# Two of seven products of a Strassen-Winograd input projection split once more, with operands kept from the first phase

## The chip, the core and the metric

The kernel runs on one core of a Trainium2 chip. TensorE (PE, with its weight loads listed as PEld) multiplies and writes PSUM; VectorE (DVE) and ScalarE (ACT) do elementwise work and are the ones that read PSUM here; GpSimd (POOL) does a few small things and issues some DMAs; SyncE (SP) only issues DMAs. The metric is the device time of one execution in microseconds (us), taken as the median of the runs.

## What is computed

The reference, cut to the one layer that runs (`DEPTH` is 1): 4096 tokens of 1024 channels, all in float32.

```python
normed = rms_norm(x, norm_w)
u, gate = jnp.split(normed @ in_w, 2, axis=-1)          # in_w is 1024 x 2048
ug = u.reshape(b, s, 4, 256)
pooled = stack([trailing_mean(ug[:, :, g], w) for g, w in enumerate((2, 4, 8, 16))]) - ug
mixed = einsum('bsgc,gcd->bsgd', pooled, group_w) + group_b
h = x + (mixed.reshape(b, s, 1024) * scale * silu(gate)) @ out_w
out = rms_norm(h, final_norm_w)
```

The kernel folds each group's map `group_w` into `in_w` beforehand, so that one projection gives the mapped values and the gates.

## The kernel before, in words

**Arithmetic.** Each matrix product is done on float32 numbers that are split into a high and a low part (`split`, line 154: ACT copies the high part, DVE subtracts it to get the low part), and three matmuls high·high, high·low, low·high make one product (`mm3`, line 576). On top of it each 2x2 block product is done by the Strassen-Winograd scheme in seven block products: P1 = A11 B11, P2 = A12 B21, P6 = S2 T2, P7 = S3 T3, P5 = S1 T1, P4 = A22 T4, P3 = S4 B22. The S are sums of blocks of A (the normalised tokens, transposed), the T sums of blocks of B (the weights).

**Stages.** There are three, each a row of steps, and a step is one product (line 960). First input phase "a": four blocks of 1024 tokens, seven products each, for the first two groups (values and gates). Second input phase "b": the same four blocks for the last two groups. Output phase "o": eight blocks of 512 tokens, seven products each. In the input phases one product is 48 matmuls (`product_in`, line 587): two halves h of 256 rows of the inner dimension, four column tiles ct of 128, two kk of 128 rows, three matmuls of 128x128 weights against 512 tokens. One (h, ct) pair, six matmuls, I call a unit. Four PSUM banks ("x") take P1, P2 and later P7, P4, the other four ("y") take P6, P5, P3.

**Operands of A.** Phase a loads the transposed tokens (`load_x`), normalises them, forms the sums (`form_in`, line 514), splits them into `op` tiles (`split_halves`, line 470), and stores the operands of P1, P2, P7 and P4 to DRAM (`sd`). Phase b loads these four back (`load_saved`, line 490) and forms the sums for P6, P5 and P3 again on DVE (`form_in` and `form_s4`): six subtractions or additions of 128x1024 a block.

**Order.** The program is written in the order of the steps; at step n the loop at line 1204 loads operands up to three steps ahead, forms sums two ahead, splits one ahead (`split_reach`), does the pooling that has come due (`pool`, line 628), runs the product (`run`, line 994), and evicts it (`evict_in`, line 710). Eviction of P1 is a copy by ACT from the x banks to the y banks, of P2, P6, P7, P3 a copy to SBUF, of P5 and P4 an addition by DVE. Each engine works through its own list in order. `tc.high_priority()` moves instructions forward in it, `tc.issue_after(...)` puts them behind another instruction. Buffers of SBUF come from a list of eleven `st` and eight `vt` tiles of 128x1024, the oldest free one first; whoever takes one waits for its last reader, DMAs included. Weights lie in `w[i][h]`; those of phase b are formed during the last block of a and the first of b (`form_wb`, `split_wb`); `make_wo` (line 320) forms those of the output phase during phase b and stores them (`wod`), `load_w` (line 328) loads and splits them in b's last block. `save_t3` (line 274), run in block 2 of phase a, loads four weight blocks, subtracts and stores T3.

Of the kernel before, what the change touches and what calls it, by code (L numbers as in the profile page):

```python
# [36 lines left out]
class Slots:  # L37
# [4 lines left out]
    def __init__(self, tiles):  # L42
        self.free = deque((0, t) for t in tiles)
        self.used = {}

# [16 lines left out]
def kernel(  # L62
# [48 lines left out]
    ops = [mem.tile([P, 4 * H], F32R, tag=f"op{i}", name=f"op{i}") for i in range(4)]  # L111
    st = Slots([mem.tile([P, D], F32, tag=f"st{i}", name=f"st{i}") for i in range(NS)])
# [41 lines left out]
    def split(dst, src):  # L154

        latest_split[1] = copy(dst[:, 0], src).ins
        latest_split[0] = sub(dst[:, 1], src, dst[:, 0].bitcast(F32)).ins
# [10 lines left out]
    wvd = [dram.tile([P, 2, H], F32, name=f"wvd{k}") for k in range(4)]  # L168
    t3d = [dram.tile([P, 2, H], F32, name=f"t3d{h}") for h in range(2)]
    wod = {  # L170
        i: [dram.tile([P, 2, H], F32, name=f"wod{i}_{h}") for h in range(2)]
        for i in range(P1, P7 + 1)
# [4 lines left out]
            for i in (P1, P2, P7, P4)  # L177
# [7 lines left out]
    nc.vector.memset(eps, EPS)  # L185
    scrap = const.tile([P, 1], F32, name="scrap")
# [133 lines left out]
    def make_wo(h):  # L320
        us = {}
        for n in range(2):
            for kh in range(2):
                us[kh, n] = load_rows(out_w, 4 * kh + 2 * h, n * H)
                scale_rows(us[kh, n], pair(scale_c, h, kh))
        store_weights(wod, h, us[0, 0], us[1, 0], us[0, 1], us[1, 1])

    def load_w(src, i):
        for h in range(2):
            u = take()  # L330
            nc.sync.dma_start(out=u, in_=src[i][h])
            split(w[i][h], u)
# [128 lines left out]
    turn = [0]  # L461

    def next_op(pattern, **sizes):
        t = ops[turn[0] % 4]
        turn[0] += 1
        return t.rearrange(pattern, **sizes)
# [3 lines left out]
    def split_halves(us, saved=None, by_pool=False):  # L470
        ts = []
        for h, u in enumerate(us):
            t = next_op("p (s a b) -> p s a b", s=2, a=2)
# [24 lines left out]
    def swapped(q, b):  # L498
        return q == 0 and b > 0

    def load_in(q, b, i):
        s = xs[b]
        if i == P1:
            s["11"] = load_saved(b, P1) if q else load_x(b, 0, 0)
        elif i == P2:
            s["12"] = load_saved(b, P2) if q else load_x(b, 0, 1)
        elif i == P7 and swapped(q, b):
            s["21"] = load_x(b, 1, 0)
        elif i == P6:
            if not swapped(q, b):  # L510
                s["21"] = load_saved(b, P7) if q else load_x(b, 1, 0)
            s["22"] = load_saved(b, P4) if q else load_x(b, 1, 1)

    def form_in(q, b, i):

        s = xs[b]
        if i in (P1, P2):
            if q == 0:
                for u in s["11" if i == P1 else "12"]:
                    normalize(b, 0, u)  # L520
        elif i == P7 and swapped(q, b):
# [4 lines left out]
        elif i == P6:  # L526
            s["2"] = [take() for _ in range(2)]
            for h in range(2):
                if q == 0:
                    normalize(b, 1, s["22"][h])  # L530
                sub(s["2"][h], s["22"][h], s["21"][h])
            if q == 0:
                give(rstd.pop(b))
# [6 lines left out]
    def split_in(q, b, i):  # L540
        s = xs[b]
        key = {P1: "11", P2: "12", P6: "2", P7: "21", P5: "11", P4: "22", P3: "12"}[i]
        later = q == 0 and b == 0 and i in (P1, P2)
        t = split_halves(s[key], None if q or later else sd[b].get(i), b == 0)
        if later:
            stores.extend(zip(sd[0][i], s[key]))
        if i == P6 and (q or b):
            form_s4(b)
        if i == P6 and swapped(q, b):
            for u in s.pop("21"):  # L550
                give(u)
        elif i not in (P1, P2, P6) and not (i == P7 and swapped(q, b)):
# [33 lines left out]

    def product_in(i, t, sets, by_bank, between=None, behind=None):
        ps = sets[bank_of[i]]
# [3 lines left out]
        for n, (h, ct) in enumerate(halves):  # L592
            if between and n in between:
                between[n]()
            c = slice(ct * P, (ct + 1) * P)
            with tc.issue_after(behind) if behind and n == 1 else nullcontext():
                for kk in range(2):
                    mm3(
                        ps[ct],
                        (w[i][h][:, 0, kk, c], w[i][h][:, 1, kk, c]),  # L600
                        (t[h][:, 0, kk], t[h][:, 1, kk]),
# [720 lines left out]
```

## Time and profile before

| | |
|---|---|
| median of 3 runs | 916.59 us (915.73 to 917.37) |
| the profiled execution | 917.32 us, of which the span from first to last instruction is 915.6 us |
| granted TensorE clock | 0.998 |
| busy: PE, DVE, ACT | 904.4 us (99%), 703.5 us (77%), 457.5 us (50%) |
| matmuls and weight loads | 4212 each |
| DMA | 177.02 MB, mean 193 GB/s |

Start times in the trace count from the start of the span. By the first start of every 48th matmul phase a begins at 33.4 us, phase b runs from 328.3 to 618.4 us and phase o until 908.6 us. One step of phase a or b takes 10.36 us.

### The profile page before, as it was taken

The numbers are of one execution on the slowest core, as the hardware profiler recorded it, in microseconds if no ns is written. First come the engines' busy times: TensorE is split into PE (matmuls) and PEld (weight loads), VectorE is DVE, ScalarE is ACT, GpSimd is POOL, SyncE is SP. The second block draws the span as 40 slices with busy tenths as digits, with TensorE's granted clock in tenths as the row PEclk, the third lists the DMA queues.
The fourth block names the chain that finished last, engine by engine and source line by source line (L and its number), as shares of the span: only waits on it lengthen the run. The fifth ranks groups of instructions, "written<-read, shape, count | busy, mean of one in ns | idle before, by whom it ended". The sixth has DMA issues, their size and how long they took to land.

```text
span 915.6 us, 11210 instructions
## 1 busy us (share of the span) xinstructions
PE 904.4 (99%) x4212; PEld 789.0 (86%) x4212; DVE 703.5 (77%) x769; ACT 457.5 (50%) x741; POOL 52.6 (6%) x130
## 2 busy tenths in 40 slices
PE   9999999999999999999999999999999999999996
PEld 7788888888888888888888888888888888888886
DVE  3898994894699997586696589589978677676675
ACT  7869447447345565246345546654423424324333
POOL 0023201001100000000000000000101101001010
PEclk9999999999999999999999999999999999999999
DMA  9986865666756635016614725745746536356122
GB/s 340 401 320 195 316 236 166 214 230 197 264 198 241 250 146 200 24 47 238 244 47 160 257 87 194 246 161 184 252 165 227 163 135 230 128 194 216 37 92 93
DMA packets 66518, 177.02 MB, mean 193 GB/s; under 512 B 6048, under 2 KB 23840, under 8 KB 66464
## 3 DMA queue, kind: packets, MB, share of 16 engines
q1 hardware_dynamic: 59888, 154.78, 47.9%
q10 hardware_dynamic: 4176, 13.65, 3.8%
q0 software_dynamic: 2400, 7.88, 2.5%
q8 instruction: 33, 0.54, 0.2%
q14 instruction: 21, 0.17, 0.1%
HBM read 115.45 MB, written 60.83 MB: 193 GB/s over the span
## 4 chain that ended last, share of the span: by engine, by line
PE 88%; DMA 5%; DVE 3%; ACT 2%; issue 1%; SPq 0%; DVEq 0%; ACTq 0%
PE bank L581 88%; DMA early<-in_wut 2%; DMA st<-in_x 1%; DMA st<-wvd 1%; DMA st<-in_xt 1%; DVE op L146 1%; DMA t3d<-st 1%; PE bank L374 0%; DVE st L146 0%; DVE st L149 0%; ACT early L408 0%; ACT op L152 0%; DVE st L143 0%; DVE vt L143 0%; DVE vt L146 0%
## 5 line engine op out<-in xcount | busy, mean ns | idle before, releaser
L581 PE MATMUL bank<-op,w 128*128 128x512 f32 x2688 | 581.8, 379 | 2.3 <-DVE op L146 1.5
L581 PEld LDWEIGHTS bank<-op,w 128*128 128x128 f32 x2688 | 507.6, 189 | 75.7 <-DVE op L146 2.3
L581 PE MATMUL bank<-w,op 128*128 128x512 f32 (+1 forms) x1356 | 290.3, 377 | 0.0
L581 PEld LDWEIGHTS bank<-w,op 128*128 128x128 f32 x1356 | 254.6, 189 | 35.8
L146 DVE TENSOR_TENSOR op<-st,op 128x1024 fp32r<-128x1024 f32 x127 | 154.6, 1221 | 75.6 <-ACT op L152 75.5
L152 ACT ACTIVATE op<-st 128x1024 fp32r<-128x1024 f32 x127 | 133.1, 1052 | 143.8 <-PE bank L581 128.5
L152 ACT ACTIVATE vt<-bank 128x512 f32<-128x512 f32 x100 | 56.8, 593 | 49.3 <-PE bank L581 42.4
L152 ACT ACTIVATE op<-vt 128x1024 fp32r<-128x1024 f32 x39 | 40.9, 1055 | 78.8 <-PE bank L581 65.7
L924 DVE TENSOR_TENSOR st<-bank,st 128x512 f32<-128x512 f32 x60 | 41.1, 687 | 29.8 <-PE bank L581 29.4
L146 DVE TENSOR_TENSOR st<-st,st 128x1024 f32<-128x1024 f32 x35 | 42.5, 1221 | 19.3 <-DMA st<-sd 8.6
L146 DVE TENSOR_TENSOR op<-vt,op 128x1024 fp32r<-128x1024 f32 x39 | 47.5, 1222 | 9.5 <-ACT op L152 9.5
L194 POOL TENSOR_SCALAR oms<-oss 128x2 f32<-128x2 f32 x14 | 9.2, 658 | 600.0 <-ACT st L813 593.9
L152 ACT ACTIVATE bank<-bank 128x512 f32<-128x512 f32 x48 | 27.8, 580 | 30.7 <-PE bank L581 27.1
L146 DVE TENSOR_TENSOR w<-st,w 128x1024 fp32r<-128x1024 f32 x21 | 25.5, 1221 | 12.4 <-ACT w L152 12.3
L662 DVE TENSOR_TENSOR_SCAN vt<-vt,bf 128x512 f32<-128x512 f32 x28 | 34.5, 1269 | 0.2 <-ACT vt L152 0.2
L143 DVE TENSOR_TENSOR vt<-bank,vt 128x512 f32<-128x512 f32 (+1 forms) x51 | 33.2, 678 | 1.6 <-PE bank L581 1.6
L924 DVE TENSOR_TENSOR vt<-bank,vt 128x512 f32<-128x512 f32 (+1 forms) x37 | 24.8, 673 | 12.0 <-PE bank L581 11.7
L152 ACT ACTIVATE w<-st 128x1024 fp32r<-128x1024 f32 x21 | 21.9, 1053 | 17.9 <-PE bank L581 14.9
L149 DVE TENSOR_TENSOR st<-st,vt 128x1024 f32<-128x1024 f32 x23 | 27.2, 1219 | 3.1 <-DMA st<-in_xt 3.1
L684 DVE SCALAR_TENSOR_TENSOR vt<-vt,vt 128x1024 f32<-128x1024 f32 x24 | 29.1, 1214 | 0.0
L152 ACT ACTIVATE st<-bank 128x512 f32<-128x512 f32 x30 | 17.5, 595 | 22.7 <-PE bank L581 10.8
L817 DVE SCALAR_TENSOR_TENSOR st<-st,ors,st 128x1024 f32<-128x1024 f32 x17 | 21.4, 1281 | 6.1 <-POOL ors L212 6.1
(130 smaller groups left out, 556.0 us busy)
## 6 DMA issues: line engine op xcount, KB each, us to landing
st<-in_x SPq DMA_DIRECT2D x36, 512.0 KB, 5.0
st<-in_xt SPq DMA_DIRECT2D x29, 512.0 KB, 6.6
st<-sd SPq DMA_DIRECT2D x29, 512.0 KB, 5.0
sd<-st ACTq DMA_DIRECT2D x23, 512.0 KB, 3.7
vt<-in_x SPq DMA_DIRECT2D x21, 512.0 KB, 5.1
st<-yd SPq DMA_DIRECT2D x19, 512.0 KB, 4.3
yd<-vt SPq DMA_DIRECT2D x18, 512.0 KB, 2.8
out<-st SPq DMA_DIRECT2D x17, 512.0 KB, 3.6
```

The source lines that it names most:

```text
L143: nc.vector.tensor_tensor(out=dst, in0=a, in1=b, op=ALU.add)
L146: return nc.vector.tensor_tensor(out=dst, in0=a, in1=b, op=ALU.subtract)
L149: nc.vector.tensor_tensor(out=dst, in0=a, in1=b, op=ALU.mult)
L152: return nc.scalar.activation(dst, src, func)
L194: nc.gpsimd.tensor_scalar(out=ms, in0=ss, scalar1=1.0 / D, scalar2=EPS, op0=ALU.mult, op1=ALU.add)
L581: latest[0] = nc.tensor.matmul(ps, a, b, start=start and n == 0, stop=stop and n == 2, skip_group_check=True).ins
L662: nc.vector.tensor_tensor_scan(s[:, j, at:end], v[:, j, at:end], v[:, j, at - win : end - win], sums_of[j] if sums_of else 0.0, ALU.add, A ...
L684: nc.vector.scalar_tensor_tensor(out=s[:, :, at : at + H], in0=s[:, :, at : at + H], scalar=1.0 / win, in1=v[:, :, HIST:], op0=ALU.mult, o ...
L817: nc.vector.scalar_tensor_tensor(out=us[j], in0=us[j], scalar=rs[:, j : j + 1], in1=fw[0], op0=ALU.mult, op1=ALU.mult,)
L924: partial["added"] = nc.vector.tensor_tensor(out=dst, in0=src, in1=dst, op=ALU.add).ins
```

## The change

Phase a stores the operands of all seven products; phase b loads all seven, two steps ahead, and `form_in` is left to phase a. `op` becomes a list of eight half-size tiles, so that high and low part lie in tiles of their own. In blocks 1 to 3 of phase b the products P1 and P7 (`INNER`) are no longer 48 matmuls: the 512x512x512 product is itself done as seven products of 256x256x256, in the order P1, P6, P2, P7, P5, P4, P3 (called inner P1 and so on here), each 12 matmuls of 128x128 weights against 256 tokens. Their intermediate sums are copied by ACT between halves of the x banks (`carry`), and one that can't be accumulated goes through DVE. The matmuls of an inner product's step are interleaved with the second half of the step before it (P3 or P6), as `fill`. The seven weight operands of each of the two are formed during phase a (blocks 1, 2) and block 0 of phase b, stored to DRAM, and loaded by POOL's queue into the memory of `w[P1]`, `w[P7]` and three `st` tiles, which are taken out of the list from block 0 of phase b until P7 of its last block. Stores of weights, and of `yd` in phase b, are kept in a list `due` and issued at the start of the next step. The diff, cut to its core:

```diff
-    ops = [mem.tile([P, 4 * H], F32R, ...) for i in range(4)]
+    ops = Slots([mem.tile([P, 2 * H], F32R, ...) for i in range(8)])
...
     def split_in(q, b, i):
         s = xs[b]
+        if q:
+            us = s[i]
+            if is_inner(b, i):
+                inner.update(us=us, sums={}, ops={})
+                with tc.high_priority():
+                    split_inner(M_ORDER[:4])
+                return None
...
+    M_ORDER = (P1, P6, P2, P7, P5, P4, P3)
+    def split_inner(ms):
...
+            if m == P6:
+                add(sums_in[P5], q[0, 1], q[1, 1])
+                sub(sums_in[P6], sums_in[P5], q[0, 0])
+            elif m == P7:
+                sub(sums_in[P7], q[0, 0], q[0, 1])
+            elif m == P3:
+                sub(sums_in[P3], q[1, 0], sums_in[P6])
...
+            split((by_side(ts[m][:, 0]), by_side(ts[m][:, 1])), src)
...
+    def mm_inner(m, banks_of, j, th):
+        t, wm = inner["ops"].pop(m), inner["w"][M_ORDER.index(m)]
+        for c in range(2):
+            ps = banks_of[2 * j + c][:, th * 256 : (th + 1) * 256].rearrange(...)
+            for kk in range(2):
+                for n, (sw, sr) in enumerate(((0, 0), (0, 1), (1, 0))):
+                    latest[0] = nc.tensor.matmul(ps, wm[:, sw, kk, cols_of], ..., start=False, ...)
+        ops.give(t)
+    def clear_inner(i, sets):
+        with tc.high_priority():
+            for v in part(sets[bank_of[i]], 0, 0):
+                copy(v, zero.to_broadcast([P, 256]))
+    def inner_product(i, sets, fill):
+        v11, v12, v21, v22 = part(ps, 0, 0), part(ps, 1, 0), part(ps, 0, 1), part(ps, 1, 1)
+        def carry(dst, src):
+            with tc.high_priority():
+                for c in range(2):
+                    inner["copied"] = copy(dst[c], src[c]).ins
+        mm_inner(P1, ps, 0, 0)
+        carry(v12, v11)
+        fill.pop(0)()
+        fill.pop(0)()
+        with tc.high_priority():
+            split_inner(M_ORDER[5:])
+        mm_inner(P6, ps, 1, 0)
+        carry(v21, v12)
+        fill.pop(0)()
+        mm_inner(P2, ps, 0, 0)
+        mm_inner(P7, ps, 0, 1)
+        u3 = inner["tiles"][0][:, 0]
+        carry(v22, v21)
+        carry([u3[:, 0], u3[:, 1]], v21)
+        fill.pop(0)()
+        mm_inner(P5, ps, 1, 1)
+        for c in range(2):
+            sub(u3[:, c], v22[c], u3[:, c])
+        mm_inner(P4, ps, 0, 1)
+        mm_inner(P3, ps, 1, 0)
+        for c in range(2):
+            add(v12[c], v12[c], u3[:, c])
...
+    def load_wi(i, ms):
+        for m in ms:
+            nc.gpsimd.dma_start(out=wi[i][m], in_=wid[i][m].bitcast(F32R))
+    def store_wi(i, src):
+        behind, after = latest_split[0], evicted[0]
+        for m, b in src.items():
+            u = take("p (s a b) -> p s a b", s=2, a=2)
+            r = u.bitcast(F32R)
+            with tc.issue_after(behind):
+                with tc.issue_after(after):
+                    copy(r[:, 0], b)
+                sub(r[:, 1], b, u[:, 0])
+            due.append((wid[i][M_ORDER.index(m)], u))
...
+        elif inner_step(n):
+            evict_in(b, 1, i, sets)
+        elif inner_step(n + 1):
+            t = split_up.pop(n)
+            clear_inner(next_i, sets)
+            for ct in range(4):
+                unit(i, t, sets, 0, ct)
+            give_ops(t[0])
+            with tc.high_priority():
+                split_inner(M_ORDER[4:5])
+            inner_product(next_i, sets, [lambda ct=ct: unit(i, t, sets, 1, ct) for ct in range(4)])
...
+            with tc.issue_after(inner["copied"]):
+                evict_in(b, 1, i, sets)
...
-        return 3 if kind == "a" and i == P6 else 4 if kind == "o" else 3
+        return 4 if kind == "o" else 3 if kind == "a" else 2
...
+    WI_PLAN = {
+        ("a", 1, P2): [(P1, 0)], ("a", 1, P6): [(P1, 1)], ("a", 1, P4): [(P1, 2)],
+        ("a", 2, P1): [(P1, 3)], ("a", 2, P7): [(P1, 4)],
+        ("b", 0, P6): [(P7, 0)], ("b", 0, P7): [(P7, 1)], ("b", 0, P5): [(P7, 2)],
+        ("b", 0, P4): [(P7, 3)], ("b", 0, P3): [(P7, 4)],
+    }
...
+        store_due()
```

`WI_PLAN` names the step behind which a part of the weights is formed: part 0 loads the raw blocks, part 1 makes four differences on DVE and stores them, parts 1 to 4 split and store the seven operands (`store_wi`). The output phase's weights are loaded one step before `split_w` splits them, and `make_wo` moves from behind P5 to behind P4, its loads staying behind P5.

More of the change, by code (lines that the diff above doesn't have):

```diff
@@ L44, in __init__, with retire, extend @@
         self.used = {}
+        self.tags = {}
+    def retire(self, n):
+        return [self.tags.pop(id(self.free.popleft()[1])) for _ in range(n)]
+    def extend(self, tiles):
+        for t, tag in tiles:
+            self.tags[id(t)] = tag
+            self.free.append((Slots.clock, t))
     def age(self):
@@ L460, with next_op, give_ops @@
     xs = [{} for _ in range(NB)]
[L461 to L466, printed above, removed]
+    def next_op(a):
+        return tuple(
+            ops.take(lambda t: t.rearrange("p (a b) -> p a b", a=a)) for _ in range(2)
+        )
+    def give_ops(ts):
+        for u in ts:
+            ops.give(u)
     first_saves = []
@@ new lines, in part @@
+    def part(ps, j, th):
+        return [ps[2 * j + c][:, th * 256 : (th + 1) * 256] for c in range(2)]
+    def clear_inner(i, sets):
[3 more added lines that the diff above has]
+    def inner_product(i, sets, fill):
+        ps = sets[bank_of[i]]
+        inner["w"] = wi[i]
+        v11, v12, v21, v22 = part(ps, 0, 0), part(ps, 1, 0), part(ps, 0, 1), part(ps, 1, 1)
[25 more added lines that the diff above has]
+            add(v12[c], v12[c], u3[:, c])
+        give(inner["tiles"][0])
@@ new lines, in store_wi, with raw_wi @@
+    def store_wi(i, src):
[8 more added lines that the diff above has]
+            due.append((wid[i][M_ORDER.index(m)], u))
+    def raw_wi(i):
+        formed["raw"] = []
+        for h in range(2):
+            if i == P1:
+                formed["raw"].append(load_rows(in_w, 2 * h, D + H))
+            else:
+                formed["raw"].append(take())
+                nc.sync.dma_start(out=formed["raw"][-1], in_=t3d[h])
@@ L632, in pool @@
         end = HIST + H
+        befores = small.tile([P, 4], F32, tag="before", name=f"bf{b}_{q}_{half}")
         for g in range(2):
@@ L1137 @@
         split_up[2] += split_halves([s["2"][h]])
+    stores.extend(zip(sd[0][P6], s["2"]))
     give(rstd.pop(0))
```

270 lines of the change are left out of this document (215 added, 55 removed).

## The prediction

> **What bounds the kernel now.** First the page's shares and its chain:
>
> ```profile
> PE 904.4 (99%) x4212; PEld 789.0 (86%) x4212; DVE 703.5 (77%) x769; ACT 457.5 (50%) x741; POOL 52.6 (6%) x130
> PE 88%; DMA 5%; DVE 3%; ACT 2%; issue 1%; SPq 0%; DVEq 0%; ACTq 0%
> ```
>
> Then the waits of PE alone, and PE's timeline, which starts a new row at each idle gap:
>
> ```profile
> PE bank L581 <- DVE op L146: 1.5, 2, 1.0
> PE bank L581 <- ACT w L224: 0.7, 1, 0.7
> ...
> 256.76 25.60 PE L581 MATMUL bank<-op,w 128*128 128x512 f32 x116 [0.96 <-DVE op L146]
> ...
> 459.83 100.53 PE L581 MATMUL bank<-op,w 128*128 128x512 f32 x465
> ```
>
> The reader is to see that TensorE is the bound. In the product line it waits 2.2 us in all, of which 0.96 us lies before 256.76, where phase a's last block begins. In 100 us of phase b it doesn't wait once. So a matmul less is time gained, and every wait put on PE is time lost; all else is worth nothing unless it makes PE wait.
>
> **PE's own work.** The tail of the kernel has both sizes of matmul, each with new weights, in two pieces of the PE timeline; their single durations are in the groups kept apart by shape:
>
> ```profile
> 899.91 5.99 PE L581 MATMUL bank<-w,op 128*128 128x512 f32 x27
> 905.74 2.84 PE L581 MATMUL bank<-w,op 128*128 128x256 f32 x24
> ...
> L581 PE MATMUL bank<-w,op 128*128 128x512 f32 x1332 | 287.7, 379 | 0.0
> ...
> L581 PE MATMUL bank<-w,op 128*128 128x256 f32 x24 | 2.8, 275 | 0.0
> ```
>
> The step from one matmul to the next is (5.99 − 0.379) / 26 = 0.2158 us at 512 tokens and (2.84 − 0.275) / 23 = 0.1115 us at 256. The weight load, which isn't shorter for 256, doesn't set the pace. A product of 48 costs 48 x 0.2158 = 10.36 us; seven inner products of 12 cost 84 x 0.1115 = 9.37 us. Gain 0.99 us each, six of them (P1 and P7, blocks 1 to 3): **−5.95 us**. All other matmuls stay.
>
> **Waits inside an inner product.** It is a chain: PE, a copy or subtraction in PSUM, PE again. Prices, and the busy time of the two steps that belong to it (P3 and P1: rows 1, 3, 5; P6 and P7: rows 2, 4, 6):
>
> ```profile
> L152 ACT ACTIVATE op<-st 128x1024 fp32r<-128x1024 f32 x127 | 133.1, 1052 | 143.8 <-PE bank L581 128.5 <-DVE st L149 14.8 <-DVE st L143 0.2
> L146 DVE TENSOR_TENSOR st<-st,st 128x1024 f32<-128x1024 f32 x35 | 42.5, 1221 | 19.3 <-DMA st<-sd 8.6 <-DMA st<-wvd 6.1 <-ACT st L232 4.3
> L152 ACT ACTIVATE bank<-bank 128x512 f32<-128x512 f32 x48 | 27.8, 580 | 30.7 <-PE bank L581 27.1 <-DVE st L146 3.6
> L844 ACT ACTIVATE st<-st 128x512 f32<-128x512 f32 x4 | 2.5, 632 | 7.1 <-DVE st L924 5.3 <-issue 1.9
> L149 DVE TENSOR_TENSOR st<-st,st 128x512 f32<-128x512 f32 x2 | 1.4, 682 | 0.0
> L924 DVE TENSOR_TENSOR vt<-bank,vt 128x256 f32<-128x256 f32 x2 | 0.8, 420 | 0.0
> L844 ACT ACTIVATE st<-vt 128x256 f32<-128x256 f32 x2 | 0.8, 408 | 0.0
> ...
> core 0: us, PE busy (x) PEld busy (x) DVE busy (x) ACT busy (x) POOL busy (x), PEclk, DMA share, GB/s
> 390.50:411.20 20.70, 20.70 (x97) 18.12 (x97) 17.59 (x23) 9.44 (x14) 0.00 (x0) 1.00 0.13 52
> 421.60:442.30 20.70, 20.70 (x97) 18.12 (x97) 12.34 (x11) 11.06 (x17) 0.00 (x0) 1.00 0.83 308
> 463.00:483.70 20.70, 20.70 (x98) 18.12 (x97) 17.21 (x17) 10.85 (x24) 0.00 (x0) 1.00 0.13 51
> 494.10:514.80 20.70, 20.70 (x97) 18.12 (x97) 8.85 (x8) 13.11 (x20) 0.00 (x0) 1.00 0.59 209
> 535.50:556.20 20.70, 20.70 (x98) 18.12 (x97) 19.01 (x19) 12.16 (x26) 0.00 (x0) 1.00 0.31 102
> 566.60:587.30 20.70, 20.70 (x98) 18.12 (x97) 14.90 (x13) 12.48 (x17) 0.00 (x0) 1.00 0.72 255
> ```
>
> Count from the first matmul of inner P1, with 1.34 us an inner product and 1.29 us a unit. The copies are priced by the 408 ns ACT row of 128x256; it reads SBUF, but at 128x512 the PSUM row (580) and the SBUF row (632) lie together. Inner P1 ends at 1.34, its results come about 0.16 later (275 ns less one step). Two copies take it to 2.3; two units cover until 3.9: spare 1.6. Inner P6 ends at 5.3, copies at 6.2; one unit covers until 6.6, where inner P2 starts: spare 0.4. Inner P7 ends at 9.2, the first two copies at 10.2; one unit covers until 10.5, where inner P5 starts: spare 0.3. The next two copies end at 11.0, inner P4 needs them at 11.9. Inner P5's last result comes at 12.0; DVE's two subtractions of 420 ns end at 12.9, inner P3 starts at 13.2: spare 0.3 if it has to wait for them. So nothing waits if ACT and DVE are free at the instant. Neither is preemptive: a 1.05 us copy or 1.22 us subtraction that has just begun overruns the spare by 0.7 or 0.9 us.
>
> How full are they? DVE gets, per inner product, seven low parts and four sums at 682 ns and four PSUM operations at 420: 7.5 + 1.7 = 9.2 us, for the two low parts of 1.22 us before: +6.7 us. In return the sums for P6, P5, P3 go, six of 1.22 us a block; two of them lie in each window. So each window gains 4.3 us of DVE work and shrinks to 10.36 + 9.37 = 19.73 us. The P6–P7 windows come to 16.6, 13.2 and 19.2: they fit. The P3–P1 windows come to 21.9, 21.5 and 23.3: over by 2.2, 1.8 and 3.6. About 10 us in them is pooling, which nobody awaits soon and which can slide into the steps around; DVE's order decides. I take 0.5 us of PE wait for each inner P1 (between none and the whole excess) and 0.13 for each inner P7: **+1.9 us**. ACT gains seven high parts at 632 ns and ten copies at 408, less two at 1,052: +6.4 us; its fullest window is then 19.5 of 19.7 (494.1, with weight scaling that the change puts a step later), others 16 to 19. That is in the same 1.9 us.
>
> What stands behind a waiting instruction: behind ACT's carry copies the high parts of the next product and P3's or P6's eviction, so DVE's low parts too; behind DVE's two subtractions the low parts of the next product. Those have five units of cover, as the second half of an operand is needed only after four units. Behind inner P3 come DVE's two additions and ACT's copies of P1 to the y banks: P2's third unit needs the third bank 2.6 us after inner P3 ends, and 0.16 + 0.42 + 0.58 is 1.2 us. Covered.
>
> The bank matters here. No row of this trace has two engines in two halves of one bank. The Trainium skill, PSUM — Partial Sum Buffer, section "PSUM bank collisions raise a hardware error", says that two engines may not be in one bank and partition quadrant at a time, at different addresses either, and that access has to be guarded by bank. By that rule inner P3, which writes the left halves of two banks, has to wait for DVE's reading of their right halves, and inner P2 for the copies into its own banks; without it only data would bind, and inner P3 wouldn't wait for DVE at all. The sum above goes by that; without it the waits of the inner P1s would be those for carry copies alone, by my estimate half, and the time about 0.8 us lower.
>
> **Phase a and the DMAs.** In transfers of 512 KB: 24 more stores (P6, P5, P3; four blocks, two halves), 24 more loads, 14 weight stores, 12 for raw blocks and differences, 26 weight loads by POOL: 100, or 52 MB on 177.
>
> ```profile
> 109.20:181.80 72.60, 72.60 (x338) 63.58 (x337) 56.55 (x58) 41.21 (x66) 5.18 (x14) 1.00 0.63 217
> 181.80:254.30 72.50, 72.50 (x337) 63.48 (x336) 50.75 (x53) 37.85 (x61) 6.01 (x14) 1.00 0.65 224
> ...
> 328.30:400.80 72.50, 72.50 (x338) 63.48 (x337) 54.54 (x59) 33.79 (x46) 0.00 (x0) 1.00 0.27 97
> 400.80:473.40 72.60, 72.60 (x338) 63.58 (x337) 52.07 (x51) 35.17 (x67) 0.00 (x0) 1.00 0.44 167
> ...
> 223.20:233.60 10.40, 10.40 (x50) 9.11 (x49) 1.36 (x2) 6.83 (x12) 0.77 (x2) 1.00 0.98 284
> 233.60:243.90 10.30, 10.30 (x49) 9.01 (x48) 7.23 (x10) 1.75 (x5) 2.19 (x5) 1.00 0.91 307
> ...
> 222.43 5.11 DMA t3d<-st
> 227.62 5.75 DMA st<-wvd
> ...
> 235.14 7.25 DMA st<-in_xt
> ...
> st<-sd SPq DMA_DIRECT2D x29, 512.0 KB, 5.0
> ...
> SPq L696 <- DVE vt L692: 87.1, 8, 35.1
> ```
>
> Phase b has room: block 1 adds 6 operand loads and up to 10 of weights, 8.4 MB in 72 us or 116 GB/s on 167, under the 308 that a stretch above shows. A load lands in 5.0 us and is now issued two steps ahead, 20 us; inner P7's last weights, loaded once inner P1 has done with the three tiles, have P2 and half of P6 as cover, 15 us for three transfers. I price them at nothing; a load that did come late would cost PE its lateness. SP stood up to 35 us behind a `yd` store (last row); moving those and the weight stores to the next step's start takes such waits away from operand loads, hidden before too: nothing. Forming the weights costs DVE 11 x 0.68 = 7.5 us and ACT about as much, in blocks with 16, 22 and 18 us of DVE idle: nothing.
>
> Phase a is tighter. Six more stores a block are 3.1 MB in 72.5 us, 43 GB/s on 217 to 233. The place is before 256.76: T3's round trip through DRAM and then the next block's tokens run one after another at DMA shares of 0.98 and 0.91. Into those 21 us fall the stores of P5 and P3, four transfers or 2.1 MB on 6.1 that they move now. Between −0.96 (the gap closes as buffers come in another order) and the stretch of the legs quoted by a third, 18.1 x 0.34 = +6.2 us; I take **+0.5 us**, near the low end, since P5's pair goes out before the worst leg.
>
> **The sum.** 917.32 − 5.95 + 1.9 + 0.5 = 913.8 for an execution like the profiled one. That one is 0.73 us above the median of the runs, so **913.0 us**.
>
> **Rivals.**
> *DVE becomes the bound at inner P1 (slower).* Place: DVE's two subtractions between inner P5 and inner P3, and the low parts ahead of them, behind pooling in DVE's order. Price: the whole excess, 2.2 + 1.8 + 3.6 = 7.6 us, with 0.4 for the inner P7s and 0.5 for phase a: 917.32 − 5.95 + 8.5 − 0.73 = 919.1. It decides from 0.99 us of wait per inner product; at half the excess the kernel is back where it was. For: the three windows above. Against: pooling is free to move, and before this change DVE was at 19.01 of 20.7 in one window and PE didn't wait.
> *Phase a's stores delay the tokens of block 3.* At the full 6.2 instead of 0.5: 913.0 + 5.7 = 918.7. For: DMA is full there, and PE already waits 0.96. Against: what goes out at 235 to 242 is one pair.
> *Everything is hidden.* 917.32 − 5.95 − 0.73 = 910.6; with the 0.96 gap gone, 909.7. For: every spare above is positive.
> *Something else is late*, weights through POOL's queue or buffers (three of eleven `st` tiles are gone): about 921, one wait of some 4 us in each of two blocks.
> That it doesn't do less on PE is no rival: 84 matmuls at the step measured in the tail.
>
> **Chances.** Forecast 0.58 (its own range 911 to 915; a twentieth of it ends within 0.2%), all hidden 0.08, DVE 0.18 (0.13 slower, 0.05 near the old time), phase a 0.12 (half and half), something else 0.04. The measurement can tell about 0.2%, 1.8 us: faster is under 914.8, slower over 918.4. Faster 0.55 + 0.08 = 0.63; same 0.03 + 0.05 + 0.06 = 0.14; slower 0.13 + 0.06 + 0.04 = 0.23. Range 910.0 to 920.5: it leaves out part of "all hidden" and the ends of the slower rivals, about 0.15.
>
> **What would show it.** Right: line 581 counts 288 matmuls fewer at 512 tokens, 504 new ones at 256 with a step near 0.11 us; PE's waits in phase b under 2 us, on carry copies and on DVE's subtraction; the gap before the last block of phase a within 1 us of what it was. Wrong: pieces of PE's timeline that end in phase b at inner P3 or P5 with over 1 us each (DVE), or a longer gap near 256 us that a DMA ended (phase a); a step of over 0.12 us for 256 tokens would take the gain itself.

## The result, and the profile after

The change makes the kernel slower: 950.78 us (median of 4 runs, 949.10 to 951.85) against 916.40 us, a ratio of 1.0373 [1.0354, 1.0392]. The forecast was 913.0 us. The profiled execution took 950.23 us, its span 948.4 us, at a mean granted clock of 0.987 (0.998 before); DMA moved 229.52 MB, 52.5 MB more, as counted.

The page's engine line and its chain of the changed kernel:

```profile
PE 909.3 (96%) x4428; PEld 795.2 (84%) x4428; DVE 723.6 (76%) x846; ACT 491.8 (52%) x849; POOL 71.1 (7%) x162
PE 59%; DVE 18%; DMA 12%; ACT 6%; issue 4%; SPq 0%; ACTq 0%; DVEq 0%
```

PE has 216 matmuls more (504 small ones for 288 large ones), but it isn't 99% busy any longer, and a third of the chain now runs through DVE, DMA and ACT. Where this happens is seen when the span is cut at the phases' first matmuls. First the kernel before (phase a's blocks 1 to 3, then phase b), then the changed one, with the three stretches of these phases in which the granted clock stood at half (columns: the stretch, its length, busy time of PE, PEld, DVE, ACT, POOL, granted clock, DMA share, GB/s):

```profile
109.20:328.30 219.10, 218.11 (x1010) 190.37 (x1009) 177.87 (x185) 117.72 (x186) 11.19 (x28) 1.00 0.64 225
328.30:618.40 290.10, 290.10 (x1346) 254.04 (x1345) 215.25 (x210) 147.64 (x252) 0.00 (x0) 1.00 0.44 157
```

```profile
108.40:336.70 228.30, 221.39 (x1009) 190.81 (x1009) 180.94 (x193) 120.02 (x195) 13.83 (x28) 0.99 0.78 277
336.70:651.40 314.70, 291.55 (x1561) 259.37 (x1560) 233.66 (x279) 179.85 (x350) 14.01 (x26) 0.97 0.72 254
...
230.85:234.26 3.41, 2.86 (x7) 2.32 (x8) 2.36 (x2) 3.41 (x6) 0.57 (x1) 0.50 0.75 256
428.82:435.65 6.83, 4.65 (x11) 3.71 (x12) 5.25 (x8) 3.08 (x11) 0.55 (x1) 0.50 0.64 227
602.90:613.14 10.24, 4.06 (x15) 3.70 (x16) 8.47 (x12) 3.89 (x6) 0.00 (x0) 0.50 0.56 200
```

Length less PE's busy time is PE's idle time. Phase b was never idle and is now idle for 314.70 − 291.55 = 23.15 us; its busy time, which should have fallen by 5.95, rose by 1.45. Phase a went from 0.99 to 6.91 us idle, and its busy time rose by 3.28 for the same matmuls. Together 23.15 + 1.45 + 5.92 + 3.28 = 33.8 us; the executions differ by 32.9. Phase o is as it was.

Of the busy time that is too long, 7.40 in b and 3.28 in a, about half is the clock. The last three rows show it: around PE's three longest waits the granted clock stands at 0.50 for 20.48 us in all, and PE is busy in 2.86 + 4.65 + 4.06 = 11.57 us of them. At half clock half of that is lost, about 5.8 us; while PE waits, the low clock costs nothing. Another 2.6 us come from how busy time is counted: the last matmul ahead of a wait counts with 0.379 us instead of its step of 0.2158, or with 0.275 instead of 0.1115, 0.163 more at each of the 16 waits in the two phases. The remaining 2.3 us, in which starts slip by less than shows as a gap, were not taken apart. So a long wait on PE costs more than itself.

The waits of PE in the changed kernel (engine, tile and line that waited, what ended it: us in all, times, longest), and the pieces of PE's timeline where phase b loses most; a piece's idle time stands ahead of it:

```profile
PE bank L706 <- ACT op L162: 10.8, 2, 8.3
PE bank L619 <- ACT bank L162: 8.6, 2, 7.5
PE bank L619 <- ACT st L162: 4.3, 3, 2.9
```

```profile
405.52 1.50 PE L706 MATMUL bank<-op,w 128*128 128x256 f32 x12
...
431.00 15.49 PE L619 MATMUL bank<-op,w 128*128 128x512 f32 x60 [7.55 <-ACT bank L162]
446.33 1.50 PE L706 MATMUL bank<-op,w 128*128 128x256 f32 x12
...
494.90 0.49 PE L706 MATMUL bank<-op,w 128*128 128x256 f32 x2 [2.50 <-ACT op L162]
...
576.83 1.60 PE L706 MATMUL bank<-op,shared_st 128*128 128x256 f32 x12 [0.70 <-DVE st L156]
...
609.08 0.79 PE L706 MATMUL bank<-op,w 128*128 128x256 f32 x2 [8.30 <-ACT op L162]
```

The first row says that PE's own gain is there: 12 matmuls at 256 tokens in 1.50 us, (1.50 − 0.275) / 11 = 0.111 us a step. Then come one wait of 7.55 us in block 1, one of 2.50 in block 2 and one of 8.30 in block 3, none at the place that I had named (inner P3 behind DVE's subtraction, where 0.70 stands). From here on "product P1" and "product P7" are the two that are done as seven, and "inner P3" and the like are the small products within one.

**The wait of block 1.** SyncE's waits from 400 to 421 us, its next two operand loads and their times to landing, then DVE and ACT:

```profile
SPq L796 <- DVE vt L948: 14.2, 2, 12.2
...
418.20 1.23 SPq L526 DMA_DIRECT2D vt<-sd  x2
...
DMA to landing us min/median/max: 7.6/8.5/9.3
```

```profile
420.04 1.22 DVE L156 TENSOR_TENSOR op<-st,op 128x1024 fp32r<-128x1024 f32 x1
428.03 0.69 DVE L153 TENSOR_TENSOR st<-vt,st 128x512 f32<-128x512 f32 x1 [6.77 <-issue]
...
429.85 0.43 DVE L153 TENSOR_TENSOR bank<-bank,st 128x256 f32<-128x256 f32 x1
```

```profile
425.86 1.06 ACT L162 ACTIVATE op<-vt 128x1024 fp32r<-128x1024 f32 x1 [4.82 <-DMA vt<-sd]
...
430.37 0.58 ACT L162 ACTIVATE bank<-bank 128x512 f32<-128x512 f32 x1 [2.77 <-DVE bank L153]
```

Read from the end: PE's unit at 431.00 waits for ACT's copy of P1 out of its bank (430.37), that copy for DVE's first addition in the bank (429.85), and that addition stands in DVE's list behind a sum of 128x512 at 428.03, one of product P7's, which `split_inner` put there with high priority. DVE did nothing for 6.77 us before it. The profile names no releaser ("issue"); the two operand loads issued from 418.20 on fit. The first landed after 7.6 us, at 425.84, and released ACT's copy at 425.86; the second, issued at 418.64, landed after 9.3 us, at 427.95, and the sum starts at 428.03. In SP's list they stand behind two stores of `yd`, which waited 14.2 us for pooling on DVE (line 948). Product P7 itself starts only at 446.33: counted to the matmul the load had 28 us, but DVE was free for the sum at 421.26, 2.6 us after the issue.

**The wait of block 3.** ACT and DVE ahead of 609.08:

```profile
589.78 1.57 ACT L162 ACTIVATE op<-st 128x1024 fp32r<-128x1024 f32 x2 [7.88 <-DMA st<-sd]
...
607.19 1.83 ACT L162 ACTIVATE op<-st 128x512 fp32r<-128x512 f32 x3 [5.37 <-DVE st L153]
```

```profile
590.87 1.83 DVE L156 TENSOR_TENSOR op<-st,op 128x1024 fp32r<-128x1024 f32 x2 [8.57 <-ACT op L162]
592.62 3.63 DVE L918 TENSOR_TENSOR_SCAN vt<-vt,bf 128x512 f32<-128x512 f32 x3
...
604.20 2.36 DVE L156 TENSOR_TENSOR w<-st,w 128x1024 fp32r<-128x1024 f32 x2
606.47 0.69 DVE L153 TENSOR_TENSOR st<-st,st 128x512 f32<-128x512 f32 x1
```

A load is late again (ACT idle 7.88 us, DVE 8.57 behind it). What DVE couldn't do then it does afterwards: from 592.62 pooling and the splits of the output phase's weights, and only at 606.47 the sum from which ACT and PE take an operand of product P7.

### The profile page after: what moved, and what is told of

Read it like the earlier page. It is cut to its first block, busy times and chain, and to the rows that moved or that the text cites. A ratio compares the mean times of both kernels' runs of the same rounds, so it can differ in the third digit from the quotient of the medians.

```text
span 948.4 us, 12129 instructions
## 1 busy us (share of the span) xinstructions
PE 909.3 (96%) x4428; PEld 795.2 (84%) x4428; DVE 723.6 (76%) x846; ACT 491.8 (52%) x849; POOL 71.1 (7%) x162
## 2 busy tenths in 40 slices
DMA packets 81180, 229.52 MB, mean 242 GB/s; under 512 B 7648, under 2 KB 25440, under 8 KB 81120
## 4 chain that ended last, share of the span: by engine, by line
PE 59%; DVE 18%; DMA 12%; ACT 6%; issue 4%; SPq 0%; ACTq 0%; DVEq 0%
PE bank L619 53%; PE bank L706 5%; DVE op L156 3%; DVE st L159 2%; DVE vt L153 2%; DVE st L156 2%; DMA early<-in_wut 2%; DMA st<-in_x 2%; DMA st<-wvd 2%; DMA sd<-st 2%; DVE st L153 1%; ACT op L162 1%; DVE vt L940 1%; DVE vt L156 1%; DMA st<-sd 1%
## 5 line engine op out<-in xcount | busy, mean ns | idle before, releaser
L619 PE MATMUL bank<-op,w 128*128 128x512 f32 x2400 | 530.6, 382 | 18.0 <-ACT bank L162 8.6
L619 PEld LDWEIGHTS bank<-op,w 128*128 128x128 f32 x2400 | 454.0, 190 | 87.2 <-ACT bank L162 9.2
L156 DVE TENSOR_TENSOR op<-st,op 128x1024 fp32r<-128x1024 f32 (+1 forms) x129 | 138.2, 1081 | 63.5 <-ACT op L162 51.7
L162 ACT ACTIVATE op<-st 128x1024 fp32r<-128x1024 f32 (+1 forms) x129 | 120.3, 942 | 124.4 <-PE bank L619 64.8
L162 ACT ACTIVATE op<-vt 128x1024 fp32r<-128x1024 f32 (+1 forms) x52 | 51.5, 995 | 81.2 <-PE bank L619 66.1
L156 DVE TENSOR_TENSOR op<-vt,op 128x1024 fp32r<-128x1024 f32 (+1 forms) x52 | 59.1, 1140 | 7.9 <-ACT op L162 7.6
L162 ACT ACTIVATE bank<-bank 128x512 f32<-128x512 f32 (+1 forms) x84 | 40.2, 488 | 35.6 <-PE bank L706 18.9
L706 PE MATMUL bank<-op,w 128*128 128x256 f32 x288 | 37.2, 282 | 12.2 <-ACT op L162 10.8
L706 PEld LDWEIGHTS bank<-op,w 128*128 128x128 f32 x288 | 36.1, 197 | 14.8 <-ACT op L162 11.6
L156 DVE TENSOR_TENSOR st<-st,st 128x1024 f32<-128x1024 f32 (+1 forms) x28 | 30.2, 1090 | 13.4 <-DMA st<-wvd 13.4
L162 ACT ACTIVATE st<-bank 128x512 f32<-128x512 f32 (+1 forms) x50 | 26.1, 547 | 24.9 <-PE bank L619 9.8
```

The lines of the kernel that those rows point to most:

```text
L156: return nc.vector.tensor_tensor(out=dst, in0=a, in1=b, op=ALU.subtract)
L162: return nc.scalar.activation(dst, src, func)
L619: latest[0] = nc.tensor.matmul(ps, a, b, start=start and n == 0, stop=stop and n == 2, skip_group_check=True).ins
L706: latest[0] = nc.tensor.matmul(ps, wm[:, sw, kk, cols_of], t[:, sr, kk].rearrange("p (s a) -> p a s", s=2), start=False, stop=kk == 1 and ...
```

## The experiments

All were timed beside the kernel before on the same chip. The theory: **feeding**. Phase b's operands are loaded too late for their first reader, which holds ACT's and DVE's lists up, and pooling that is put off comes ahead of the inner products' sums. The rivals: **the inner chain itself** (DVE's subtraction, copies in the banks) and **the extra traffic**, stores in phase a and forming the weights. The edits also change which buffer an operation gets and the order of DVE's list, so that their gains can't be added. The last two columns are the lengths of phase a's blocks 1 to 3 and of phase b by their first matmuls; before they are 219.1 and 290.1, after 228.3 and 314.7. "Others" marks kernels that multiply by other values than the reference's.

| run | us | ratio to before | a | b |
|---|---|---|---|---|
| e1 no inner products | 921.90 | 1.0046 [1.0027, 1.0064] | 224.8 | 290.1 |
| e2 weights not formed (others) | 937.33 | 1.0218 [1.0191, 1.0245] | 223.2 | 305.6 |
| e3 three operands not stored (others) | 941.82 | 1.0265 [1.0249, 1.0281] | 220.9 | 313.9 |
| e4 loads three ahead | 940.28 | 1.0256 [1.0238, 1.0275] | 228.4 | 304.3 |
| e5 e2 to e4 together (others) | 934.85 | 1.0193 [1.0178, 1.0209] | 218.8 | 308.3 |
| e6 loads in POOL's queue | 954.04 | 1.0412 [1.0394, 1.0429] | 227.0 | 318.0 |
| e7 pooling behind the product | 940.95 | 1.0257 [1.0228, 1.0286] | 230.3 | 304.0 |
| e8 e1, T3 stored a block earlier | 921.43 | 1.0055 [1.0037, 1.0074] | 222.5 | 290.1 |
| e9 e5, blocks 1 and 2 alone (others) | 917.84 | 1.0008 [0.9999, 1.0018] | 218.4 | 289.9 |
| e10 e9 with e7 for e4 (others) | 917.78 | 1.0017 [1.0007, 1.0028] | 217.8 | 290.9 |
| e11 e4 without output weights (others) | 936.80 | 1.0219 [1.0201, 1.0238] | 227.9 | 299.3 |
| e12 e4, blocks 1 and 2 alone (others) | 928.89 | 1.0132 [1.0112, 1.0152] | 228.6 | 292.2 |

**e1: the stores and loads alone.**

```diff
-        return b > 0 and i in INNER
+        return False
...
-        for what, k in WI_PLAN.get((kind, b, i), ()):
-            form_wi(what, k)
```

(and nothing takes or loads the inner weights).

> The first part of the change alone: phase a stores all seven operands, phase b loads all seven two steps ahead, no inner products, no weights for them, all eleven st tiles. In the changed kernel phase a's blocks 1 to 3 took 228.3 us (219.1 before) and phase b 314.7 us (290.1 before). Theory 'buffers and late loads' (operand loads of phase b land late because the inner products' weights take three tiles and their operands hold others): phase b back at 290 to 292 us. Rival 'two steps ahead is too late in itself': phase b stays above 300. For phase a, theory 'the added stores' keeps about 228 us, theory 'forming the inner weights' gives about 219. So about 917 us if both are with the inner products, about 926 if the stores cost phase a its 9 us.

1.0046: 4.9 us lost, all in phase a (5.7 there in the profiled execution, which lies 0.9 above the median); phase b is exactly as long as before, so seven loads a block, two steps ahead, hurt nothing by themselves. Phase a came out between the two values expected. PE's timeline of e1, and its chain ahead of the waits:

```profile
255.88 0.48 PE L619 MATMUL bank<-op,w 128*128 128x512 f32 x1 [1.74 <-ACT op L162]
257.96 365.52 PE L619 MATMUL bank<-op,w 128*128 128x512 f32 x1679 [1.60 <-DVE op L156]
```

```profile
215.72 4.52 DMA sd<-st
...
220.37 5.00 DMA st<-wvd
...
226.71 5.55 DMA t3d<-st
...
232.28 8.83 DMA st<-wvd
...
242.83 7.05 DMA st<-in_xt
```

This is the place and the mechanism of the phase-a rival: T3's round trip. The weight load with which it begins goes out only when a store of operands has landed, 2.6 us later than before (220.37 against 217.79), and the one behind T3's store takes 8.83 us instead of 5.75. The rival's price was 6.2 and the loss is 224.8 − 219.1 = 5.7, but that they lie so close is in part luck: PE's idle time rose by only 2.6 us, and the rest is the granted clock, at 0.50 from 256.98 to 263.80, where PE was busy for 5.84 us and lost half of them. The rival had no term for that.

**e2: the inner weights are not formed.** POOL loads other data of the same size in their place.

```diff
-            nc.gpsimd.dma_start(out=wi[i][m], in_=wid[i][m].bitcast(F32R))
+            nc.gpsimd.dma_start(out=wi[i][m], in_=in_w[m * P : (m + 1) * P, 0:D].rearrange(...).bitcast(F32R))
...
-        for what, k in WI_PLAN.get((kind, b, i), ()):
-            form_wi(what, k)
```

> The changed kernel without forming the inner products' weights: they are loaded from in_w instead, so the values are others. Theory 'forming the inner weights costs phase a its 9 us': blocks 1 to 3 of phase a near 219 us, time 938 to 942. Theory 'the added stores': phase a near 228 us and the time within 3 us of 950.8. Phase b: the two long waits in blocks 1 and 3 (7.6 and 8.3 us) stay by the theory of late loads; only block 0's end can gain.

5.1 us less in phase a, 9.1 less in phase b. Forming, which I had at nothing, isn't free in either. I had expected block 1's long wait to stay. It went: the sum of product P7 still stands ahead of the additions on DVE, but DVE waits only 3.25 and 1.38 us for the loads, and PE's longest wait there is 1.47 us. Block 3's stayed, 8.47 us.

**e3: P6, P5 and P3 are not stored in phase a;** phase b loads operands that are there in their place, just as many.

```diff
-            s[i] = load_saved(b, i)
+            s[i] = load_saved(b, {P6: P7, P5: P1, P3: P2}.get(i, i))
...
-        t = split_halves(s[key], None if later else sd[b][i], b == 0)
+        t = split_halves(s[key], None if later or i in (P6, P5, P3) else sd[b][i], b == 0)
```

> The changed kernel without the added stores of P6, P5 and P3 in phase a; phase b loads the stored operands of P7, P1 and P2 in their place, so the values are others. Theory 'the added stores cost phase a': blocks 1 to 3 near 219 us, time near 942. Theory 'forming the inner weights': phase a stays above 225 us and the time within 3 us of 950.8.

7.4 us less in phase a, phase b nearly the same. With e2 and e3 both (e5) phase a is back at 218.8: its loss is stores and forming, and the two overlap.

**e4: operands loaded three steps ahead, as in phase a.**

```diff
-        return 4 if kind == "o" else 3 if kind == "a" else 2
+        return 4 if kind == "o" else 3
```

> The changed kernel with phase b's operands loaded three steps ahead instead of two. Theory 'late loads' (SP issues a load only when it comes to it and the buffer is free, and the landing then heads ACT's and DVE's lists): the waits of 7.6 us in block 1 and 8.3 us in block 3 go, phase b falls by 8 to 18 us, time 933 to 943. Rival 'no buffer is free any earlier': the loads are issued when they were, time within 3 us of 950.8. Rival 'DVE is the bound': the same, within 3 us.

10.4 us less in phase b by one number, with no work taken out. PE's timeline of e4, its gaps over 1.5 us in blocks 1 to 3:

```profile
493.18 0.94 PE L706 MATMUL bank<-op,shared_st 128*128 128x256 f32 x6 [1.52 <-DVE st L156]
...
558.06 0.49 PE L706 MATMUL bank<-op,w 128*128 128x256 f32 x2 [1.65 <-ACT op L162]
568.65 0.94 PE L706 MATMUL bank<-op,shared_st 128*128 128x256 f32 x6 [1.66 <-DVE st L156]
...
598.45 0.79 PE L706 MATMUL bank<-op,w 128*128 128x256 f32 x2 [5.63 <-ACT op L162]
```

Block 1's wait of 7.55 is gone, as the late load lets one expect. The edit alone doesn't prove it: in e4 DVE also makes the two additions (421.37) ahead of the sum (423.43), the other way around than in the changed kernel. e2 speaks for the load too: there the sum stays ahead, its load comes earlier, and the wait goes. Block 3's wait is 5.63 instead of 8.30.

**e5: the three together.**

> The inner products with what feeds them made cheap: no forming of their weights (loaded from in_w), no added stores in phase a (operands of P7, P1, P2 loaded for P6, P5, P3), loads three steps ahead; values are others. What is left in phase b is the chain of inner products itself, ACT's and DVE's work and the buffers. Phase b would be 284.1 us with no wait. Theory 'the loss of phase b is late operands and weights': 286 to 292, time 913 to 920. Rival 'DVE and its order (pooling and weight splits ahead of the inner sums) remain': 296 to 304, time 923 to 932, with the long wait at inner P7 of block 3 still there.

308.3 us in phase b, 4 more than e4 alone with less work: above both ranges expected, and against the theory that late operands and weights are the whole loss. PE's longest gap in e5, and DVE ahead of it:

```profile
592.57 7.49 PE L706 MATMUL bank<-op,w 128*128 128x256 f32 x36 [10.00 <-ACT op L162]
```

```profile
589.09 0.69 DVE L153 TENSOR_TENSOR st<-st,st 128x512 f32<-128x512 f32 x1 [3.39 <-DMA yd<-st]
```

Block 3 again: the tile that the sum is to go into is still being stored to `yd`, 3.39 us of the 10.00. When a buffer comes free counts here, and any edit deals the buffers out anew.

**e6: the same loads, in POOL's queue instead of SP's.**

```diff
-            nc.sync.dma_start(out=u, in_=sd[b][i][h])
+            nc.gpsimd.dma_start(out=u, in_=sd[b][i][h])
```

> The changed kernel with phase b's operand loads issued on POOL's queue instead of SP's, still two steps ahead. Theory 'SP's list': the loads stand behind yd, wod and weight stores and loads on SP, so on POOL's queue they go out earlier and phase b falls by 5 to 15 us (time 936 to 946). Rival 'buffers': the load waits for a buffer whichever queue issues it, within 3 us of 950.8.

3.3 us worse than the changed kernel in phase b, so taking the loads out of SP's list, from behind the `yd` stores, doesn't help by itself. POOL's queue in block 1 of e6 shows why:

```profile
416.62 0.54 POOL L526 DMA_DIRECT2D vt<-sd  x1 [12.43 <-DVE vt L159]
418.22 0.54 POOL L526 DMA_DIRECT2D vt<-sd  x1 [1.06 <-DVE vt L940]
419.43 0.54 POOL L526 DMA_DIRECT2D vt<-sd  x1 [0.67 <-DVE vt L948]
```

The three loads still go out between 416 and 420 us, each when an instruction of pooling on DVE is done with a `vt` tile. So in this block the buffer held them, and pooling held the buffer; SP's list is only another thing that waits for the same pooling.

**e7: in phase b, pooling that is due is written behind the step's product.**

```diff
-        pool_due(n)
+        if kind != "b":
+            pool_due(n)
...
         run(n)
+        if kind == "b":
+            pool_due(n)
```

> The changed kernel with phase b's pooling put behind the step's product in program order, so that the inner products' splits, subtractions and additions on DVE stand before it. Theory 'pooling ahead on DVE' (the wait of 2.5 us at inner P1 of block 2 has 5.5 us of pooling ahead of the split): phase b falls by 5 to 12 us. Rival 'buffers and late loads': pooling frees buffers, later pooling frees them later, so phase b stays within 3 us or gets longer.

10.7 us less in phase b, as much as e4. PE's timeline of e7, one gap of block 1 and one of block 3:

```profile
422.87 1.60 PE L706 MATMUL bank<-op,shared_st 128*128 128x256 f32 x12 [1.76 <-DVE st L156]
...
597.58 0.49 PE L706 MATMUL bank<-op,w 128*128 128x256 f32 x2 [2.10 <-ACT op L162]
```

The 8.30 us at product P7 of block 3 have become 2.10 when pooling is put behind the sums; as pooling also frees buffers, the run doesn't say how much of that is DVE's order. What is left in block 1 is the wait that I had forecast, at inner P3.

**e8: e1 with T3 stored in block 1 instead of block 2** (`b == 2` becomes `b == 1` in the condition of `save_t3`).

> The first part alone (as e1) with the subtraction for T3 and its round trip through DRAM done in block 1 of phase a instead of block 2. e1 lost 5.7 us in phase a, all at its last block's start. Theory 'the added stores lengthen T3's round trip, and the next tokens' loads stand behind it on SP' : phase a back to 219 to 221 us, time 915 to 918. Rival 'DMA is simply full there': the loss moves or stays, time 920 to 924.

Phase a 222.5, 2.3 less than e1, but the loss reappears a block earlier: 2.02 us ahead of 184.77, where block 2 begins, with 3.41 us at half clock behind it. So the rival held. The whole stayed the same (1.0055 against 1.0046).

**e9: e5, with inner products in blocks 1 and 2 alone.** The memory of the inner weights is given back a block earlier.

```diff
-        return b > 0 and i in INNER
+        return 0 < b < NB - 1 and i in INNER
```

> As e5 (weights not formed, fewer stores, three ahead; values are others), with inner products in blocks 1 and 2 only; phase b without a wait would be 286.1 us. In e5 block 3 held some 13 us of waits and a stretch of slow clock behind the longest. Theory 'block 3 is its own case (weight splits, pooling and buffers together)': phase b 290 to 295 us, time 917 to 921. Rival 'the waits move to block 2': above 300 us.

The same time as before, 1.0008. Phase b of e9, and the only two gaps of PE in it:

```profile
327.60:617.50 289.90, 286.82 (x1490) 255.44 (x1489) 211.07 (x237) 166.66 (x310) 10.80 (x20) 1.00 0.67 233
```

```profile
470.38 1.49 PE L706 MATMUL bank<-op,w 128*128 128x256 f32 x11 [0.60 <-DVE op L156]
482.30 1.60 PE L706 MATMUL bank<-op,shared_st 128*128 128x256 f32 x12 [2.48 <-DVE st L156]
```

Four inner products should bring 3.96 us. PE's busy time fell by 3.28; 3.08 of idle time ate it. Both gaps belong to product P1 of block 2. DVE ahead of the second:

```profile
478.43 1.22 DVE L945 SCALAR_TENSOR_TENSOR vt<-vt,vt 128x1024 f32<-128x1024 f32 x1
479.56 1.22 DVE L156 TENSOR_TENSOR op<-st,op 128x1024 fp32r<-128x1024 f32 x1
480.70 1.22 DVE L159 TENSOR_TENSOR vt<-vt,vt 128x1024 f32<-128x1024 f32 x1
481.83 0.75 DVE L156 TENSOR_TENSOR st<-bank,st 128x256 f32<-128x256 f32 x2
```

Two pooling steps and a low part stand ahead of the two subtractions, and inner P3 starts when the first of them is done, though it doesn't use their result: it writes the other half of the bank that they read. The Trainium skill, PSUM — Partial Sum Buffer, section "PSUM bank collisions raise a hardware error", asks for a guard by bank; here, where the program's semaphores keep to that, it costs 2.48 us in one place.

**e10: e9 two steps ahead, with e7's order.**

> As e9, with loads two steps ahead and pooling behind the step's product in program order (values are others). Theory 'what is left is pooling ahead of the inner sums on DVE': phase b 286 to 290 us, time 912 to 916, and at last faster than before. Rival 'the subtraction and the bank': waits at inner P3 stay at 1 to 2 us each, phase b 290 to 296, time 916 to 922.

1.0017, and the rival's ranges held. PE's gaps in phase b are 1.14, 0.38 and 1.81 us, again all in product P1 (two of them at inner P3): with pooling written last it still gets between.

**e11: e4 without loading and splitting the output phase's weights in block 3.** Phase o so multiplies by what lies there.

```diff
-                split_w(i)
-                if i != P3:
-                    load_w(wod, ORDER_IN[ORDER_IN.index(i) + 1])
```

> As e4 (three ahead), but the output phase's weights are neither loaded nor split in phase b's last block, so the output phase works with what lies in those tiles and its values are others. Theory 'weight loads and splits in front of the inner sums on ACT and DVE cause the long wait at inner P7 of block 3' (5.6 us in e4): it falls below 1.5 us, phase b from 304.3 to 294 to 299, time 930 to 936. Rival 'pooling and the buffer its store frees': the wait stays above 4 us.

5.0 us less than e4 in phase b. Block 3's longest gap is 3.63 instead of 5.63, between what the theory and its rival had: the weights are a part of it, not all.

**e12: e4 with e9's edit.** Contrary to its expectation not all values are the reference's: block 3's P1 and P7 multiply by inner weights that still lie in `w[P1]` and `w[P7]`.

> The changed kernel with loads three steps ahead and inner products in blocks 1 and 2 only: all values are computed. e4's phase b took 304.3 us, with about 10 us of waits and 3 us of slow clock in block 3; two products of 0.99 us of gain go with them. Expected phase b 292 to 295, phase a 228 as before, time 928 to 932. If the waits move on to block 2: 935 or more.

12.1 us less than e4 in phase b: inner products in block 3 cost that much. Phase a's 228.6 stay, so the kernel is 1.3% slower.

## Why the prediction was wrong, step by step

- **PE's own work, −5.95.** Right: the step is 0.111 us, and in e9, where little disturbs it, busy time falls by 3.28 of 3.96.
- **Waits inside an inner product, +1.9.** The place was right for product P1, the size was not. With the feeding cheap, e9 and e10 wait 3.1 and 3.3 us in two blocks, about 1.6 us a product P1 against 0.5, and nothing at product P7 against 0.13. I let pooling "slide into the steps around" because nobody awaits it soon; DVE took it first all the same. This is the DVE rival. What was measured lies between its price, 7.6 us in three blocks or 2.5 each, and mine, and alone it takes the gain of e9 and e10 to about nothing.
- **"Phase b has room … I price them at nothing."** This is the step that failed: phase b, which should have become 4 us shorter, is 24.6 us longer, and most of that lies here. I had compared bandwidth (the DMA share in b is 0.72, so there was room), taken 5.0 us for a landing and counted a load's 20 us to the matmul. But an inner product's operand is first read by DVE's sums, over a step and a half before, with high priority; the load can't go out before pooling has let go of its buffer (block 1 of e6), and the two that were late took 7.6 and 9.3 us to land. I had also counted on SP's list to be free of waits with the `yd` stores moved to the next step's start; it still stood 12.2 us at one of them. When it is late, everything behind its reader in ACT's and DVE's lists is late, among it the copies that free PE's banks. Giving the load more lead took 10.4 us off (e4), putting pooling last 10.7 (e7), not forming the weights 9.1 (e2); these overlap. That late operands and weights are not all of it is what e5 shows: with all of them made cheap, block 3 still waits 10.00 us. "Something else is late" had two waits of 4 us and a chance of 0.04; the waits were 7.55 and 8.30, and the clock fell during both.
- **What stands behind a waiting instruction.** I had listed the copies of P1 to the y banks as covered, on the assumption that DVE's additions come in time. The 7.55 us lie at just that copy.
- **Forming the weights, "nothing".** Wrong: 5.1 us in phase a by e2. No run separates what of it is work on DVE and ACT and what is loads, stores and buffers.
- **Phase a, +0.5.** The rival with T3's round trip was right in its place; its price (6.2 forecast, 5.7 by e1) was right with the help of the clock, as said at e1. I had chosen the low end of a range because P5's stores go out before the worst leg; in e1 the trip already starts late, behind a store of operands. With forming the whole is 9.2.
- **The clock.** No term of the sum: about 5.8 us of the 32.9. In the phases of the trace before, PE's longest wait was 0.96 us, and the clock didn't fall.

What stays open: how the loss of block 3, the largest of the blocks, divides between late buffers, pooling and the output weights (e5, e7 and e11 each move it, and not by sums); and how much of inner P3's wait would be left if the bank were free, which was not tried.

No version here beats the kernel before; the best, e9 (1.0008) and e10 (1.0017), come to within 0.2% of it, and they leave out work that the change needs.

## What to carry to other kernels

Count a load's lead to its first reader in the longest list, a sum or a split, not to the matmul, and from the moment when its buffer is let go, not from its place in the program. Then ask what stands behind that reader: an instruction at high priority that waits for late data stops an engine that works in order. On a kernel whose bound is 99% busy, a gain of 1 us per product pays only if the helpers' added work has a place of its own; that nobody waits for other work soon doesn't keep it out of the way. Free bandwidth says nothing of when a buffer comes free.

## What the runs showed of the hardware

- **The clock falls by stretches, not by single waits.** In these traces the granted clock of the three phases is 1 or 0.50, and within a trace it changes only at whole multiples of 3.41 us; a fall lasts one to four such stretches (3.41, 6.83, 10.24 and 13.65 us). It fell behind every stretch in which PE was idle for 2.02 us or more, behind none with 1.79 or less, and behind two of five in between. So where a wait lies counts as much as its length. Two waits at the same place show it, one of 2.88 us in the changed kernel and one of 2.82 in e11. These are the stretches in which they begin:

```profile
227.44:230.85 3.41, 1.08 (x6) 0.60 (x4) 0.00 (x0) 0.10 (x1) 0.00 (x0) 1.00 1.04 302
...
227.13:230.54 3.41, 1.61 (x8) 1.07 (x6) 0.00 (x0) 0.00 (x0) 0.00 (x0) 1.00 1.12 351
```

  In the first PE is idle for 2.33 us and the next stretch runs at 0.50; in the second the wait reaches over the border, 1.80 us are idle, and the clock stays. The Trainium skill, TensorE: Matmul & The Clock Gate, section "Part 1: The HAM clock gate", has half clock after an idle window of about 3.4 us and full clock after as long a busy one. The traces agree with the 3.4 us, but a window in which PE was idle for only 2.13 us was enough (e8, 181.93 to 185.34).
- **A DMA's time depends on what runs beside it.** The load of a weight block of 512 KB behind T3's store took 5.75 us before and 8.83 us in e1. The DMA engines were fully busy meanwhile in both (shares of 0.99 and 1.03), though phase a's mean is 0.64 and 0.74; a phase's mean share doesn't tell how long a load takes.
- **Two engines in one bank.** By the program's semaphores inner P3 waits for DVE's reading of the other half of its banks: 2.48 us in e9, 1.52 and 1.66 in e4. What two accesses at once would do, no run here shows.
